# The copy ahead of the second slab's cast, other pairs in the first group, and sums called at the fetch, in a macaron encoder kernel

## The chip, the cores and the metric

The kernel runs on one core of a Trainium2 chip. The metric is device time in microseconds (us) of one execution. A core has TensorE (PE) for matmuls, VectorE (DVE), ScalarE (ACT), GpSimd (POOL) and SyncE (SP). Each engine works through its own list of instructions in order and waits for the others by semaphores. SP and POOL are used here to issue DMA transfers.

## What is computed

The reference is a two-layer encoder trunk. Each layer has a feed-forward block, a mixer and a second feed-forward block, so there are four feed-forward blocks, called (0,0), (0,1), (1,0) and (1,1) by layer and place. The change touches the feed-forward blocks alone:

```python
D_MODEL, SEQ, N_META, D_FF, DEPTH = 1024, 512, 16, 2816, 2

def swiglu(x, w_gate, w_up, w_down):
    return (jax.nn.silu(x @ w_gate) * (x @ w_up)) @ w_down

for l in range(DEPTH):
    h = h + 0.5 * swiglu(rmsnorm(h, norm_gains[l, 0]), ffn_w_gate[l, 0], ffn_w_up[l, 0], ffn_w_down[l, 0])
    h = h + mixer(...)
    h = h + 0.5 * swiglu(rmsnorm(h, norm_gains[l, 2]), ffn_w_gate[l, 1], ffn_w_up[l, 1], ffn_w_down[l, 1])
```

There are 528 tokens (16 of them learned), 512 behind the last mixer, so a half of the tokens is 264 or 256 columns.

## The kernel before

**Tiling.** The 2816 hidden channels are 22 chunks of 128, taken as 11 pairs. The pairs stand in groups of 4, 4 and 3 (`GROUPS`). Activations lie with channels on partitions and tokens along the row.

**Seven products instead of eight.** A pair's gate and up projections are written as a 2x2 block product and computed with seven products, named 1 to 7, in the order 1, 2, 6, 5, 7, 4, 3. Products 1, 2 and 4 use a weight block as it lies in memory, products 6, 5, 7 and 3 use sums of blocks. The down projections of the first two groups (`SEVENS = 2`) are done in the same way: `seven(g, what)` runs products 1, 6, 5, 7, 4, 2, 3 for two pairs of the group, the pairs whose hidden tensors were turned into the operand forms by `forms`. The group's other two pairs are multiplied plainly (`o22`, `o21`, `ea`, `eb`). The loads of such a group carry the numbers 11 and 12 (`NPAIR + g`). Each product is 24 matmuls.

**Weights.** A weight slab is a 128x1024 fp32 tile. SP fetches it into one of three `wraw` buffers. `make` turns it into two tiles: ACT casts it to `whi` (L305) and DVE subtracts to get the remainder `wlo` (L306), four buffers each. A matmul with full accuracy is three: hi by hi, hi by lo, lo by hi. Slabs that are sums are put together by `sums`: ACT writes a negative (`s`, L251), SP loads a plain block into a `wsb` buffer, and POOL issues DMAs that add onto a tile (L256). For the slab of product 6 there are two such additions, one behind the other: memory onto `s`, then `s` onto `w`.

**Partial sums.** A pair's quarters collect in the tile `c` (two buffers). After products 1, 6 and 7, `snapshot` copies the PSUM tile to `c` on ACT (L705), and the next product that adds onto that PSUM tile must wait for the copy. Products 2, 5 and 3 are added by DVE (L710). `hidden` then scales (L736, L739, DVE), applies silu (ACT L465), multiplies (L740), and either splits the result into hi and lo (`split`, L470 and L471) or, for the pairs in `SUMMED`, calls `forms` (ACT L755 and L764, DVE L756 to L765).

**The order at a group's end.** The last pair's product 7 is followed by the group's product 1, then by the pair's products 4 and 3, then by the group's products 6, 5, 7, `o22`, 4, `o21`, `ea`, 2, `eb` and 3. Product 4 adds onto the tile that the snapshot of product 7 reads. The additions to `h` (L803, DVE) take the group's results from PSUM.

The framework orders each engine's list by priority and readiness. `self.after(self.behind)` is a queueing rule alone: the cast is placed on ACT's list behind the instruction `behind`. Before the change it is used for one slab of block (0,0) and for the slabs in `RESERVED`.

In block (0,0) the first two pairs, 0 and 1, go through `first_pair` (eight plain products while the inputs arrive), and all their `hidden` steps run at once behind them.

Of the kernel before, what the change touches and what calls it, by code (L numbers as in the profile page):

```python
# [17 lines left out]
P = 128  # L18
# [15 lines left out]
SLAB = 1024  # L34
# [8 lines left out]
GROUPS = (4, 4, 3)  # L43
SEVENS = 2
# [19 lines left out]
RESERVED = [((l, f), 1, "5") for l, f in ((0, 1), (1, 0), (1, 1))]  # L64
SQUARES = {(0, "2"): (0, 1, 2, 3), (1, "1"): (4, 5, 6, 7)}
EARLIEST = ((0, 0), 2, "1")
SUMMED = [sum(GROUPS[:g]) + i for g in range(SEVENS) for i in range(2)]
LATE = KC - 3
PLACE = {p: i for i, p in enumerate("1256743")}
BLOCKS = ("11", "12", "21", "22")  # L70
# [3 lines left out]
NPAIR = FF // P // 2  # L74
# [143 lines left out]
class Weights:  # L218
# [58 lines left out]
    def fetch(self, upto):  # L277

        while self.fetched < min(upto, len(self.loads)):
            load = self.loads[self.fetched]  # L280
            if isinstance(load, int):
                w = self.raw.tile([P, SLAB], F32, tag="raw", name=f"raw{load}")
                self.nc.sync.dma_start(w, self.wts[load])
                self.raws[self.fetched] = w
            elif load[2] in DIRECT:
                w = self.raws[self.fetched] = self.block(*load[:2], DIRECT[load[2]])
                if load == EARLIEST:
                    self.sums(*load, w)
            self.fetched += 1

    def make(self, upto):
        nc = self.nc
        while self.made < min(upto, len(self.loads)):
            self.fetch(self.made + 1)
            s = self.made
            load = self.loads[s]
            w = self.raws.pop(s, None)
            if w is None:
                w = self.summed.pop(load)
            hi = self.hi_pool.tile([P, SLAB], F32R, tag="whi", name=f"whi{s}")  # L300
            lo = self.lo_pool.tile([P, SLAB], F32R, tag="wlo", name=f"wlo{s}")
            for a in np.split(np.arange(SLAB), 2 if s == 0 else 1):
                cs = slice(a[0], a[-1] + 1)
                with self.after(self.behind if load == ((0, 0), 2, "6") or load in RESERVED else None):
                    nc.scalar.copy(hi[:, cs], w[:, cs])  # L305
                nc.vector.tensor_tensor(lo[:, cs], w[:, cs], hi[:, cs].bitcast(F32), ALU.subtract)  # L306
            self.got[s] = (hi, lo)
            self.got.pop(s - 12, None)
            self.made += 1
            if not isinstance(load, int) and load[2] in ("1", "2") and load != EARLIEST:  # L310
                self.sums(*load, w)

    def use(self, j):
# [31 lines left out]
def build(tc, ctx, xt, wts, win, wdn, par, w2, const, umask, out):  # L345
# [118 lines left out]
    def act(*args, **kw):  # L464
        prev_act[0] = S.activation(*args, **kw).ins  # L465

    def split(src, tag_hi, tag_lo):
        n = src.shape[-1]
        hi, lo = slot(tag_hi, F32R, n), slot(tag_lo, F32R, n)
        S.copy(hi, src)  # L470
        V.tensor_tensor(lo, src, hi.bitcast(F32), ALU.subtract)  # L471
        return hi, lo
# [153 lines left out]
    def ffn(l, f, norm, done, following):  # L626

        x, rs, n = norm.x, None, live[0]
        w = n // 2
        pools = kept.pop() if kept else open_pools("left", psum=("s2",), c=2, gx=6, s2=2)  # L630
        made, hid, sums, formed, sevens = {}, {}, {}, {}, {}

        def second(p):
            return (p + f) % 2 == 0

        def quarters():
            return slots["c"].tile([P, 4 * T], F32, tag="c", name=nm("c"))[:, : 4 * n].rearrange("p (j q c) -> p j q c", j=2, q=4)
# [61 lines left out]
        def finished(p, product):  # L699
            st = made[p]  # L700
            acc = st[{"2": "Y", "5": "Z", "3": "Z"}.get(product, "X")][:, :, :w]

            def snapshot(q):
                with tc.high_priority():
                    snap = S.copy(st["c"][:, :, q], acc).ins  # L705
                if p == 0 and q == 3:
                    W.behind = snap

            def more(q, acc):
                V.tensor_tensor(st["c"][:, :, q], st["c"][:, :, q], acc, ALU.add)  # L710

            if product == "1":
                st["c"] = quarters()
                snapshot(0)
            elif product == "2":
                more(0, acc)
            elif product == "6":
                snapshot(1)
            elif product == "7":
                snapshot(3)  # L720
                more(3, st["Z"][:, :, :w])
            elif product == "4":
                hidden(st, p, 1)
            elif product == "3":
                more(1, acc)
                hidden(st, p, 0)

        def hidden(st, p, m):

            c = st["c"]  # L730
            t, u = [c[:, j, 2 * m : 2 * m + 2].rearrange("p q c -> p (q c)") for j in range(2)]
            x21 = st["X"][:, :, :w] if "X" in st else None
            cuts = [(t, u, t, u, slice(0, n))] if m == 0 or x21 is None else \
                [(t[:, :w], u[:, :w], x21[:, 0], x21[:, 1], slice(0, w)), (t[:, w:], u[:, w:], t[:, w:], u[:, w:], slice(w, n))]
            for td, _, ts, _, cs in cuts:
                V.scalar_tensor_tensor(td, ts, -0.5, rs[:, cs], ALU.mult, ALU.mult)  # L736
            act(t, t, AF.Silu)
            for _, ud, _, us, cs in cuts:
                V.scalar_tensor_tensor(ud, us, -0.25, rs[:, cs], ALU.mult, ALU.mult)  # L739
                V.tensor_tensor(ud, t[:, cs], ud, ALU.mult)  # L740
            if p in SUMMED:
                st["rows"] = st.get("rows", 0) + 1
                if st["rows"] == 2:
                    formed[p] = forms(c)
            else:
                hid[2 * p + m] = split(u, "g", "g")

        def forms(c):

            t, u = c[:, 0], c[:, 1]  # L750
            two = [[v2(slot(tag, F32R)) for _ in range(2)] for tag in ("g", "g", "gx")]
            last = v2(slot("gx", F32R))

            def parts(to, src):
                S.copy(to[0], src)  # L755
                V.tensor_tensor(to[1], src, to[0].bitcast(F32), ALU.subtract)  # L756

            parts(two[0], u[:, 0:4:2])
            V.tensor_tensor(t[:, 0:4:2], u[:, 1:2].broadcast_to([P, 2, w]), u[:, 0:4:3], ALU.subtract)
            V.tensor_tensor(t[:, 1], u[:, 3], t[:, 0], ALU.subtract)  # L760
            parts(two[1], t[:, 0:2])
            V.tensor_tensor(t[:, 3], u[:, 2], t[:, 1], ALU.subtract)
            parts(two[2], t[:, 2:4])
            S.activation(last[:, 0], u[:, 3], AF.Copy, scale=-1.0)  # L764
            V.scalar_tensor_tensor(last[:, 1], u[:, 3], -1.0, last[:, 0].bitcast(F32), ALU.mult, ALU.subtract)  # L765
            return [(hi[:, i], lo[:, i]) for hi, lo in two for i in range(2)] + [(last[:, 0], last[:, 1])]

        def seven(g, what):

            base, (left, right) = sum(GROUPS[:g]), (slice(0, w), slice(w, n))  # L770
            alone = second(base + GROUPS[g] - 1)
            st = sevens.setdefault(g, {})

            def weights(name):
# [6 lines left out]

            def times(to, half, name, wt, begin=False):
                hi, lo = wt
                for k in range(2):
                    xh, xl = formed[base + k][PLACE[name]]
                    for j in range(2):
                        for i, (a, b) in enumerate(((hi, xh), (hi, xl), (lo, xh))):
                            TE.matmul(to[:, j], a[:, 2 * half + j, k], b, start=begin and k == 0 and i == 0,  # L788
                                      stop=k == 1 and i == 2, skip_group_check=not begin)

            def plain(to, hs, wt, begin=False):
                hi, lo = wt
                for k in range(4):
                    xh, xl = hid[2 * base + 4 + k]
                    for j in range(2):
                        for i, (a, b) in enumerate(((hi, xh), (hi, xl), (lo, xh))):
                            TE.matmul(to[:, j], a[:, j, k], b[:, hs], start=begin and k == 0 and i == 0,  # L797
                                      stop=k == 3 and i == 2, skip_group_check=not begin)
# [14 lines left out]
            elif what == "5":  # L813
                wt = weights(what)
                for half in range(2):
                    z = acc("z", half, alone)
                    times(z, half, what, wt, True)
                    add(z, half, 0, right)
# [609 lines left out]
    first = Norm(G_NORM)  # L1428
# [16 lines left out]
    for l in range(DEPTH):  # L1445
        a, b, c = norms[3 * l : 3 * l + 3]
# [92 lines left out]
```

## Time and profile before

| | us |
|---|---|
| time, median of 3 runs | 2244.19 (2242.94 to 2246.18) |
| time of the profiled execution | 2241.11 |
| its span, first to last instruction | 2239.3 |
| PE busy / DVE busy / ACT busy | 2183.8 / 1611.1 / 1267.9 |
| PE idle behind ACT's copy at L705 | 37.1 in 9 waits |

The span is covered by the trace; 1.8 us of the profiled execution's time lie around it. Matmuls overlap in the pipe, so a matmul's own duration (287 ns) is longer than the distance from one to the next, and busy time of PE is not a measure of its speed. The granted clock of TensorE is given as a share: 1.00 is 2.4 GHz, 0.50 is 1.2 GHz.

### The profile page before, as it was taken

To read this page: it belongs to the slowest core of one execution; us is meant where nothing else is said; L and a number is where in the kernel's file an instruction comes from. 1 tells how busy PE (TensorE), PEld (TensorE's weight loads), DVE (VectorE), ACT (ScalarE), POOL (GpSimd) and SP (SyncE) were. 2 spreads that over 40 slices of the span, in tenths; PEclk is the share of its full clock that TensorE was granted. 3 is DMA by queue.
4 is the path that set the end of the run, shared out by engine and by line. 5 is a ranking of instruction groups with operands and counts; after the bars stand their busy time and mean duration, and the time that the engine had idled before them with its cause. 6 is when DMAs were issued, how large, how long until landed. Compare 5 with 4: busy or idle time off the path is not lost. (4 is left out here: it accounts for less than half of the span.)

```text
span 2239.3 us, 40811 instructions
## 1 busy us (share of the span) xinstructions
PE 2183.8 (98%) x16764; PEld 2104.0 (94%) x16764; DVE 1611.1 (72%) x2599; ACT 1267.9 (57%) x1892; POOL 175.6 (8%) x204
## 2 busy tenths in 40 slices
PE   9899999999999999999999999999999999899998
PEld 9899999999999999999998999999888889899997
DVE  7858567577876696685797586675889867768675
ACT  8546355354784574554585463554557937646454
POOL 1011110000000011111011111100000001111110
PEclk9999999999999999999999999999999999999999
DMA  8589673212114585878677796732221137878671
GB/s 247 144 214 220 156 180 114 83 60 63 42 38 128 137 225 155 223 170 209 175 187 193 192 223 160 189 117 82 75 67 48 66 113 179 217 187 229 165 193 66
DMA packets 93338, 332.05 MB, mean 148 GB/s; under 512 B 10336, under 2 KB 12640, under 8 KB 93152
## 3 DMA queue, kind: packets, MB, share of 16 engines
q1 hardware_dynamic: 62272, 221.35, 28.6%
q0 software_dynamic: 28800, 104.87, 26.3%
q10 hardware_dynamic: 2080, 3.23, 0.4%
q8 instruction: 131, 2.15, 0.4%
q14 instruction: 55, 0.45, 0.1%
HBM read 274.88 MB, written 2.10 MB: 124 GB/s over the span
## 5 line engine op out<-in xcount | busy, mean ns | idle before, releaser
L695 PE MATMUL ss<-xc,whi 128*128 128x264 f32 (+1 forms) x4608 | 853.1, 287 | 37.2 <-ACT c L705 37.1
L695 PEld LDWEIGHTS ss<-xc,whi 128*128 128x128 f32 x4608 | 725.1, 192 | 40.1 <-ACT c L705 39.6
L695 PE MATMUL ss<-xc,wlo 128*128 128x264 f32 (+1 forms) x2304 | 659.2, 286 | 0.0
L306 DVE TENSOR_TENSOR wlo<-w,whi 128x1024 fp32r<-128x1024 f32 (+1 forms) x259 | 315.2, 1217 | 207.8 <-ACT whi L305 207.3
L695 PEld LDWEIGHTS ss<-xc,wlo 128*128 128x128 f32 x2304 | 440.9, 191 | 0.0
L305 ACT CAST whi<-w 128x1024 fp32r<-128x1024 f32 (+1 forms) x259 | 269.9, 1045 | 229.5 <-PE ss L695 114.4
L482 PE MATMUL mm<-x,whi 128*128 128x264 f32 (+1 forms) x1712 | 383.3, 314 | 0.0
L482 PEld LDWEIGHTS mm<-x,whi 128*128 128x128 f32 x1712 | 278.2, 188 | 15.7 <-DVE x L471 0.2
L482 PE MATMUL mm<-x,wlo 128*128 128x264 f32 (+1 forms) x856 | 264.4, 313 | 0.0
L305 ACT CAST whi<-raw 128x1024 fp32r<-128x1024 f32 x126 | 132.0, 1048 | 152.6 <-PE mm L482 69.5
L306 DVE TENSOR_TENSOR wlo<-raw,whi 128x1024 fp32r<-128x1024 f32 x126 | 153.9, 1222 | 80.1 <-ACT whi L305 79.0
L797 PE MATMUL ss<-g,whi 128*128 128x264 f32 (+1 forms) x1024 | 186.6, 283 | 0.0
L251 ACT ACTIVATE s<-w 128x1024 f32<-128x1024 f32 x100 | 106.0, 1060 | 132.0 <-DMA w<-win 83.0
L306 DVE TENSOR_TENSOR wlo<-s,whi 128x1024 fp32r<-128x1024 f32 x100 | 122.2, 1222 | 71.9 <-ACT whi L305 70.7
L305 ACT CAST whi<-s 128x1024 fp32r<-128x1024 f32 x100 | 105.1, 1051 | 115.9 <-PE ss L695 75.6
L482 PEld LDWEIGHTS mm<-x,wlo 128*128 128x128 f32 x856 | 159.6, 188 | 7.4
L797 PEld LDWEIGHTS ss<-g,whi 128*128 128x128 f32 x1024 | 158.2, 188 | 0.0
L482 PE MATMUL ss<-g,whi 128*128 128x264 f32 (+1 forms) x828 | 153.1, 301 | 0.0
L797 PE MATMUL ss<-g,wlo 128*128 128x264 f32 (+1 forms) x512 | 145.0, 283 | 0.0
L482 PEld LDWEIGHTS ss<-g,whi 128*128 128x128 f32 x828 | 120.5, 188 | 5.2
L710 DVE TENSOR_TENSOR c<-c,ss 128x528 f32<-128x528 f32 (+1 forms) x126 | 87.8, 697 | 41.5 <-ACT c L705 33.2
L256 POOL DMA_DIRECT2D w<-win x42 | 37.0, 880 | 953.5 <-DVE g L1346 386.5
(314 smaller groups left out, 3900.4 us busy)
## 6 DMA issues: line engine op xcount, KB each, us to landing
w<-win SPq DMA_DIRECT2D x217, 512.0 KB, 5.5
raw<-wts SPq DMA_DIRECT2D x126, 512.0 KB, 3.5
w<-s POOLq DMA_DIRECT2D x50, 512.0 KB, 6.1
s<-w POOLq DMA_DIRECT2D x50, 512.0 KB, 7.1
w<-win POOLq DMA_DIRECT2D x42, 512.0 KB, 8.1
s<-win POOLq DMA_DIRECT2D x42, 512.0 KB, 6.2
w<-wdn SPq DMA_DIRECT2D x40, 512.0 KB, 4.4
woa<-wdn SPq DMA_DIRECT2D x8, 512.0 KB, 6.6
```

Source lines behind the costliest of these rows:

```text
L251: self.nc.scalar.activation(t, w, AF.Copy, scale=-1.0)
L256: self.nc.gpsimd.dma_start(t, src, accum_op=ALU.add)
L305: nc.scalar.copy(hi[:, cs], w[:, cs])
L306: nc.vector.tensor_tensor(lo[:, cs], w[:, cs], hi[:, cs].bitcast(F32), ALU.subtract)
L482: TE.matmul(acc.half[i][:width], lhs, rhs[:, acc.spans[i]], start=first, stop=last)
L695: TE.matmul(acc[:, j], a[:, j, k], b[:, at], start=bool(begin and k == 0 and i == 0), stop=k == len(x) - 1 and i == 2, skip_group_check=no ...
L710: V.tensor_tensor(st["c"][:, :, q], st["c"][:, :, q], acc, ALU.add)
L797: TE.matmul(to[:, j], a[:, j, k], b[:, hs], start=begin and k == 0 and i == 0, stop=k == 3 and i == 2, skip_group_check=not begin)
```

## The change

The diff has three edits. First, `fetch` calls `sums` for product 1 of the down projections' slabs, where `make` called it. Second, at the end of each of the first two groups of every block, `behind` is set to the copy of the last pair's product 7, and the cast of the slab of the group's product 6 is placed behind it on ACT. Third, in group 0 of block (0,0) the seven products take pairs 1 and 2 instead of 0 and 1, and pairs 0 and 3 are multiplied plainly; the weights in memory are laid out to match.

```diff
--- before.py
+++ after.py
@@ -64,7 +64,18 @@
 RESERVED = [((l, f), 1, "5") for l, f in ((0, 1), (1, 0), (1, 1))]
 SQUARES = {(0, "2"): (0, 1, 2, 3), (1, "1"): (4, 5, 6, 7)}
 EARLIEST = ((0, 0), 2, "1")
-SUMMED = [sum(GROUPS[:g]) + i for g in range(SEVENS) for i in range(2)]
+
+
+def summed_pairs(block, g):
+    first = sum(GROUPS[:g]) + (block == (0, 0) and g == 0)
+    return [first, first + 1]
+
+
+def plain_pairs(block, g):
+    base = sum(GROUPS[:g])
+    return [p for p in range(base, base + GROUPS[g]) if p not in summed_pairs(block, g)]
+
+
 LATE = KC - 3
 PLACE = {p: i for i, p in enumerate("1256743")}
 BLOCKS = ("11", "12", "21", "22")
@@ -284,7 +295,7 @@
                 self.raws[self.fetched] = w
             elif load[2] in DIRECT:
                 w = self.raws[self.fetched] = self.block(*load[:2], DIRECT[load[2]])
-                if load == EARLIEST:
+                if load == EARLIEST or load[1] >= NPAIR and load[2] == "1":
                     self.sums(*load, w)
             self.fetched += 1
 
@@ -294,6 +305,7 @@
             self.fetch(self.made + 1)
             s = self.made
             load = self.loads[s]
+            summed_first = not isinstance(load, int) and load[1] >= NPAIR and load[2] == "6"
             w = self.raws.pop(s, None)
             if w is None:
                 w = self.summed.pop(load)
@@ -301,13 +313,13 @@
             lo = self.lo_pool.tile([P, SLAB], F32R, tag="wlo", name=f"wlo{s}")
             for a in np.split(np.arange(SLAB), 2 if s == 0 else 1):
                 cs = slice(a[0], a[-1] + 1)
-                with self.after(self.behind if load == ((0, 0), 2, "6") or load in RESERVED else None):
+                with self.after(self.behind if load == ((0, 0), 2, "6") or load in RESERVED or summed_first else None):
                     nc.scalar.copy(hi[:, cs], w[:, cs])
                 nc.vector.tensor_tensor(lo[:, cs], w[:, cs], hi[:, cs].bitcast(F32), ALU.subtract)
             self.got[s] = (hi, lo)
             self.got.pop(s - 12, None)
             self.made += 1
-            if not isinstance(load, int) and load[2] in ("1", "2") and load != EARLIEST:
+            if not isinstance(load, int) and load[2] in ("1", "2") and load != EARLIEST and (load[1] < NPAIR or load[2] == "2"):
                 self.sums(*load, w)
 
     def use(self, j):
@@ -703,7 +715,7 @@
             def snapshot(q):
                 with tc.high_priority():
                     snap = S.copy(st["c"][:, :, q], acc).ins
-                if p == 0 and q == 3:
+                if q == 3 and (p == 0 or p + 1 in (sum(GROUPS[: g + 1]) for g in range(SEVENS))):
                     W.behind = snap
 
             def more(q, acc):
@@ -738,7 +750,7 @@
             for _, ud, _, us, cs in cuts:
                 V.scalar_tensor_tensor(ud, us, -0.25, rs[:, cs], ALU.mult, ALU.mult)
                 V.tensor_tensor(ud, t[:, cs], ud, ALU.mult)
-            if p in SUMMED:
+            if any(p in summed_pairs((l, f), g) for g in range(SEVENS)):
                 st["rows"] = st.get("rows", 0) + 1
                 if st["rows"] == 2:
                     formed[p] = forms(c)
@@ -767,8 +779,8 @@
 
         def seven(g, what):
 
-            base, (left, right) = sum(GROUPS[:g]), (slice(0, w), slice(w, n))
-            alone = second(base + GROUPS[g] - 1)
+            left, right = slice(0, w), slice(w, n)
+            alone = second(sum(GROUPS[: g + 1]) - 1)
             st = sevens.setdefault(g, {})
 
             def weights(name):
@@ -781,8 +793,8 @@
 
             def times(to, half, name, wt, begin=False):
                 hi, lo = wt
-                for k in range(2):
-                    xh, xl = formed[base + k][PLACE[name]]
+                for k, p in enumerate(summed_pairs((l, f), g)):
+                    xh, xl = formed[p][PLACE[name]]
                     for j in range(2):
                         for i, (a, b) in enumerate(((hi, xh), (hi, xl), (lo, xh))):
                             TE.matmul(to[:, j], a[:, 2 * half + j, k], b, start=begin and k == 0 and i == 0,
@@ -790,8 +802,8 @@
 
             def plain(to, hs, wt, begin=False):
                 hi, lo = wt
-                for k in range(4):
-                    xh, xl = hid[2 * base + 4 + k]
+                for k, c in enumerate(2 * p + i for p in plain_pairs((l, f), g) for i in range(2)):
+                    xh, xl = hid[c]
                     for j in range(2):
                         for i, (a, b) in enumerate(((hi, xh), (hi, xl), (lo, xh))):
                             TE.matmul(to[:, j], a[:, j, k], b[:, hs], start=begin and k == 0 and i == 0,
@@ -1499,14 +1511,14 @@
     for l in range(DEPTH):
         for f in range(2):
             for g in range(SEVENS):
-                p = sum(GROUPS[:g])
+                own, rest = summed_pairs((l, f), g), plain_pairs((l, f), g)
                 for row in range(2):
                     for c in range(2):
-                        parts.append(dn[l, f, p : p + 2, c, :, :, row].transpose(1, 2, 0, 3).reshape(P, SLAB))
+                        parts.append(dn[l, f, own][:, c, :, :, row].transpose(1, 2, 0, 3).reshape(P, SLAB))
                 for row in (1, 0):
                     for half in range(2):
                         js = slice(2 * half, 2 * half + 2)
-                        parts.append(dn[l, f, p + 2 : p + 4, :, :, js, row].transpose(2, 3, 0, 1, 4).reshape(P, SLAB))
+                        parts.append(dn[l, f, rest][:, :, :, js, row].transpose(2, 3, 0, 1, 4).reshape(P, SLAB))
     wdn = np.ascontiguousarray(np.stack(parts))
     par = np.zeros((P, NPAR), np.float32)
     par[:, G_NORM:G_GN] = a["norm_gains"].reshape(-1, P).T
```

**Where instructions stand.** All eight group ends change alike; this is ACT's list at the end of group 1 of block (0,0). `w_00_12_2569` is the slab of product 6 (`w_00_12_2499` in the changed kernel), `w_00_12_2572` that of product 5, `s_00_12_2566` that of product 7. Before:

```order
L470 CAST g_2604<-c_2175 128x528
L305 CAST whi_2667<-w_00_12_2569 128x1024
L705 COPY c_2428<-ss_2399 128x2x264
L305 CAST whi_2699<-w_00_12_2572 128x1024
L305 CAST whi_2740<-s_00_12_2566 128x1024
```

After:

```order
L482 CAST g_2604<-c_2175 128x528
L717 COPY c_2428<-ss_2399 128x2x264
L317 CAST whi_2667<-w_00_12_2499 128x1024
L317 CAST whi_2699<-w_00_12_2502 128x1024
L317 CAST whi_2740<-s_00_12_2496 128x1024
```

The copy of product 7 and the cast have changed places. DVE's list at the same place, before:

```order
L306 TENSOR_TENSOR wlo_2668<-w_00_12_2569,whi_2667 128x1024
L803 TENSOR_TENSOR h<-h,ss_2671 128x2x264
L710 TENSOR_TENSOR c_2428<-c_2428,ss_2608 128x2x264
L803 TENSOR_TENSOR h<-h,ss_2685 128x2x264
L306 TENSOR_TENSOR wlo_2700<-w_00_12_2572,whi_2699 128x1024
L736 SCALAR_TENSOR_TENSOR c_2428<-c_2428,rs_711 128x264
L739 SCALAR_TENSOR_TENSOR c_2428<-c_2428,rs_711 128x264
```

After:

```order
L722 TENSOR_TENSOR c_2428<-c_2428,ss_2608 128x2x264
L748 SCALAR_TENSOR_TENSOR c_2428<-c_2428,rs_711 128x264
L815 TENSOR_TENSOR h<-h,ss_2671 128x2x264
L318 TENSOR_TENSOR wlo_2668<-w_00_12_2499,whi_2667 128x1024
L815 TENSOR_TENSOR h<-h,ss_2685 128x2x264
L318 TENSOR_TENSOR wlo_2700<-w_00_12_2502,whi_2699 128x1024
L751 SCALAR_TENSOR_TENSOR c_2428<-c_2428,rs_711 128x264
```

Three small instructions now stand ahead of the subtraction for slab 6: the addition to `c`, one scaling and one addition to `h`.

In block (0,0), behind the first two pairs, ACT's list before reads as follows (`c_310` is pair 0, `c_566` pair 1, `c_847` pair 2; `g_774` to `gx_780` are the forms of pair 0):

```order
L305 CAST whi_819<-w_00_2_639 128x1024
L755 CAST g_774<-c_310 128x528
L305 CAST whi_850<-w_00_3_649 128x1024
L305 CAST whi_887<-s_00_2_338 128x1024
L755 CAST g_776<-c_310 128x528
L755 CAST gx_778<-c_310 128x528
L465 ACTIVATE c_566<-c_566 128x528
L764 ACTIVATE gx_780<-c_310 128x264
L705 COPY c_847<-ss_818 128x2x264
```

After (`c_837` is pair 2):

```order
L482 CAST g_770<-c_310 128x528
L317 CAST whi_809<-w_00_2_639 128x1024
L482 CAST g_778<-c_310 128x528
L317 CAST whi_840<-w_00_3_649 128x1024
L477 ACTIVATE c_566<-c_566 128x528
L717 COPY c_837<-ss_808 128x2x264
```

Two instructions for pair 0 are gone, and one cast of a slab has moved behind the copy. At the end of that group the forms of pair 2 appear around the cast of slab 6 (`whi_1221`); after:

```order
L767 CAST g_1144<-c_837 128x528
L717 COPY c_972<-ss_943 128x2x264
L317 CAST whi_1221<-w_00_11_1043 128x1024
L767 CAST g_1146<-c_837 128x528
L767 CAST gx_1148<-c_837 128x528
L317 CAST whi_1253<-w_00_11_1046 128x1024
L776 ACTIVATE gx_1150<-c_837 128x264
```

Where before ACT had the cast, the copy and the next cast there, three of the four instructions of the forms on ACT now stand behind the cast of slab 6. On SP and POOL every row keeps its place, and so do all ACT rows at L251, which the first edit is about; the lists of the changed kernel are the same on all five engines with the first edit and without it.

## Rows read from the trace of the kernel before

**Rows 1.** The page's head: span, busy time, share of the span and instructions by engine.

```profile
span 2239.3 us, 40811 instructions
PE 2183.8 (98%) x16764; PEld 2104.0 (94%) x16764; DVE 1611.1 (72%) x2599; ACT 1267.9 (57%) x1892; POOL 175.6 (8%) x204
```

**Rows 2.** Waits of PE: engine, line, releaser; us in total, times, longest.

```profile
PE ss L695 <- ACT c L705: 37.1, 9, 6.0
PE ss L1057 <- DVE t L1066: 2.0, 2, 1.0
```

**Rows 3.** Timeline of PE: start, us, instruction, [idle before <- releaser]; five of nine waits.

```profile
64.58 0.51 PE L695 MATMUL ss<-xc,whi 128*128 128x264 f32 x2 [3.86 <-ACT c L705]
...
101.35 0.51 PE L695 MATMUL ss<-xc,whi 128*128 128x264 f32 x2 [3.08 <-ACT c L705]
...
230.50 0.81 PE L695 MATMUL ss<-xc,whi 128*128 128x264 f32 x2 [3.24 <-ACT c L705]
...
1957.82 0.58 PE L695 MATMUL ss<-xc,whi 128*128 128x256 f32 x1 [5.98 <-ACT c L705]
...
2085.99 0.39 PE L695 MATMUL ss<-xc,whi 128*128 128x256 f32 x1 [3.26 <-ACT c L705]
```

**Rows 4.** Windows of 9 us behind the nine waits: us, engines busy, PEclk, DMA.

```profile
64.58:73.58 9.00, 9.00 (x61) 9.00 (x62) 8.61 (x12) 5.55 (x8) 0.88 (x1) 0.81 0.42 125
101.35:110.35 9.00, 9.00 (x73) 9.00 (x74) 8.97 (x16) 4.84 (x6) 0.88 (x1) 1.00 0.20 61
230.50:239.50 9.00, 9.00 (x52) 9.00 (x53) 7.33 (x13) 2.85 (x4) 0.88 (x1) 0.68 0.18 60
862.11:871.11 9.00, 9.00 (x53) 9.00 (x54) 7.44 (x13) 2.96 (x4) 0.86 (x1) 0.69 0.17 60
993.96:1002.96 9.00, 9.00 (x61) 9.00 (x62) 8.34 (x14) 3.90 (x5) 0.44 (x1) 0.81 0.19 60
1224.03:1233.03 9.00, 9.00 (x53) 9.00 (x54) 7.45 (x13) 2.97 (x4) 0.86 (x1) 0.70 0.18 58
1356.23:1365.23 9.00, 9.00 (x63) 9.00 (x64) 8.55 (x15) 4.10 (x6) 0.88 (x1) 0.84 0.17 58
1957.82:1966.82 9.00, 9.00 (x55) 9.00 (x56) 7.52 (x13) 3.10 (x4) 0.86 (x1) 0.69 0.17 59
2085.99:2094.99 9.00, 9.00 (x63) 9.00 (x64) 8.37 (x15) 4.07 (x6) 0.86 (x1) 0.81 0.18 58
```

**Rows 5.** Waits of ACT for a DMA, then ACT's timeline at 228 us.

```profile
ACT whi L305 <- DMA w<-s: 54.2, 8, 8.5
...
228.90 1.04 ACT L305 CAST whi<-w 128x1024 fp32r<-128x1024 f32 x1 [5.91 <-DMA w<-s]
229.85 0.59 ACT L705 COPY c<-ss 128x528 f32<-128x528 f32 x1
```

**Rows 6.** Windows behind the copy at 230 us: the third busy time is DVE's.

```profile
229.98:234.84 4.86, 4.34 (x19) 4.34 (x20) 4.86 (x7) 1.41 (x2) 0.00 (x0) 0.50 0.02 3
236.19:236.99 0.80, 0.80 (x8) 0.80 (x8) 0.77 (x2) 0.80 (x2) 0.00 (x0) 0.99 0.81 328
237.09:245.43 8.34, 8.34 (x71) 8.34 (x70) 8.09 (x13) 4.83 (x7) 0.88 (x1) 1.00 0.39 64
```

**Rows 7.** Block (0,0) behind pairs 0 and 1: timeline of DVE and ACT.

```profile
57.83 1.32 DVE L740 TENSOR_TENSOR c<-c 128x528 f32<-128x528 f32 x2
...
63.47 0.42 DVE L765 SCALAR_TENSOR_TENSOR gx<-c,gx 128x264 fp32r<-128x264 f32 x1
...
63.92 0.60 ACT L705 COPY c<-ss 128x528 f32<-128x528 f32 x1 [0.66 <-DVE gx L765]
```

**Rows 8.** Block (0,0), end of group 0: the cast of slab 6, and POOL's additions.

```profile
99.76 1.04 ACT L305 CAST whi<-w 128x1024 fp32r<-128x1024 f32 x1 [5.72 <-DMA w<-s]
...
84.14 1.23 POOL L256 DMA_DIRECT2D s<-wdn  x1
95.11 0.87 POOL L256 DMA_DIRECT2D w<-s  x1 [9.74 <-DMA s<-wdn]
```

## Prediction

> **What bounds the kernel now.** Read the head of the page first [rows 1]: PE is busy for 2183.8 of 2239.3 us, and no other engine comes near. So time is won only where PE stands still or runs slowly. The waits of PE say where it stands still [rows 2]: 37.1 us in nine waits, all at product 4 or a like product for ACT's copy at L705; the next entry is 2.0 us. The timeline places them [rows 3]: one at 64.58 us, behind the first two pairs of block (0,0), and eight at the ends of the groups with seven products, two in each block, of 3.08 to 5.98 us. Then read the granted clock behind each wait [rows 4]. In eight of the nine windows of 9 us it is 0.68 to 0.84 instead of 1.00: for 2.9 to 5.8 us TensorE runs at its lower level, 1.2 GHz, although it is busy throughout. A wait here costs its idle time and, behind it, 9 x (1 - clock) us of work not done. Only the wait of 3.08 us, at 101.35, has 1.00 behind it.
>
> Why does the copy come late? ACT's own waits show it [rows 5]: eight casts wait 54.2 us together for the DMA that adds `s` onto `w`, which is slab 6. At 228 us the cast stands ahead of the copy, waits 5.91 us for the landing, and the copy runs 0.95 us behind the cast's start. Its source, product 7, had long been done. PE needs the copy at once, and slab 6 two products later.
>
> **The first edit** (sums called at the fetch) moves nothing: no row of ACT, POOL or SP changes place through it. I cost it at 0, and no cover is needed.
>
> **The second edit, at seven group ends** (all but the first of block (0,0)). Three terms.
>
> *Waits that go.* Behind the swap the copy needs product 7 alone, which ends while PE still works through the group's product 1. So 37.1 - 3.86 - 3.08 = 30.2 us of idle time go [rows 2, 3].
>
> *Clock that stays up.* The seven windows from 230.50 on give 9 x (0.32 + 0.31 + 0.19 + 0.30 + 0.16 + 0.31 + 0.19) = 16.0 us [rows 4].
>
> *What is late next.* The landing of slab 6 does not move. At 230.50 it lay 1.70 us ahead of PE's restart (228.80, 0.10 ahead of the cast), that is, a wait of i us has the landing i - 1.7 us behind the moment at which product 4 could have begun; call this T. DVE begins slab 6's subtraction 1.18 us behind the landing (229.98, where the first window begins) [rows 6]. From there to the end of the subtraction for `o22` it had 4.86 + 0.77 + 8.09 = 13.7 us of work in the three windows [rows 6]. Three of these instructions now stand ahead of it (an addition to `c`, one to `h`, a scaling), about 0.62 + 0.62 + 0.35 us by their spacing, which leaves 12.1. So that tile is ready at T + i - 1.7 + 1.2 + 12.1 = T + i + 11.6. PE comes there behind five products (4, 3, 6, 5, 7) of 24 matmuls at 0.12 us (8.34 us for 71, a row at full clock [rows 6]), 14.4 us, and needs the remainder at its third matmul, T + 14.6. What remains of each wait is therefore i - 3.0 us: from 0.2 us (i = 3.24) to 3.0 us (i = 5.98). Over the seven this is 30.2 - 7 x 3.0 = 9.2 us, a queue on DVE where it had been a wait for ACT. It should come in pieces: product 5 needs PSUM that DVE's additions to `c` give back, `o22` the subtraction. Slab 6 itself is subtracted at T + i + 0.7 and wanted at T + 6.0, so it is late only by 0.7 us in the worst place, and this is within the 3.0.
>
> Queued behind the copy on ACT are the casts of slabs 6, 5 and 7. None could start before the landing or before PE gives buffers back, so the copy costs them nothing; its cover is the wait for the landing itself. Should the landing come before product 7 ends, the cast would be late by the 0.59 us of the copy.
>
> Sum: 30.2 + 16.0 - 9.2 = 37.0 us.
>
> **The third edit, in block (0,0).** *Behind the first pairs.* The wait of 3.86 us ends with a copy at 63.92 that waits for the last reader of pair 0's tile, DVE's instruction at 63.47, the last of the forms [rows 7]. With pair 0 split plainly, DVE's list from 57.83 has five instructions of that size up to the last reader, at their spacing of 0.62 us: 60.9. One silu stands between on ACT, then the copy of 0.60: done at 61.9 instead of 64.5. So 2.6 us of the 3.86 go, and 1.3 remain. The lower clock behind it cost 9 x 0.19 = 1.7 us [rows 4], and I take it as gone. Together 4.3 us. Bounds: 0 if another reader holds the tile, 3.86 + 1.7 = 5.6 if the copy is early enough.
>
> *At the end of group 0.* The 3.08 us go, with no clock to win. But the forms of pair 2 now lie there: behind the cast of slab 6 ACT has two casts of forms, the cast of slab 5 and one more form, and DVE's subtraction for slab 6 stands behind the last of them. That puts 1.04 + 2 x 0.6 + 1.0 + 0.4 + 0.35 = 4.0 us between the landing and the subtraction, where elsewhere there are 1.2. The landing was at 99.66 [rows 8]. It can move by 0 to 4.3 us with PE; I take 3.4, near the upper end, since its chain starts at casts and subtractions that run earlier too. T then is 101.35 - 3.08 - 4.3 = 94.0, and the landing 2.3 us behind it. Here both additions to `h` stand ahead, so DVE's work is 12.1 - 0.6 = 11.5, and the tile for `o22` is ready at T + 2.3 + 4.0 + 11.5 = T + 17.8 against T + 14.6: 3.2 us late. The last split of pair 3 lies four small instructions and a subtraction further down DVE's list, about 4.2 us, where PE has 2.8 us of matmuls to do: 1.4 us more. So 4.6 us of new waits stand against 3.1: a loss of 1.5 us. If the landing does not move, the loss is 4.9; if nothing is late, a gain of 3.1.
>
> **The sum.** 37.0 + 4.3 - 1.5 = 39.8 us. The profiled execution took 2241.1 us, 1.8 around its span; the change makes it 2201.3. The median of the runs lies 3.1 us above the profiled execution, so I predict 2204 us. With no new wait anywhere, the gain is 30.2 + 16.0 + 4.3 + 3.1 = 53.6 us: 2191.
>
> **The rivals.**
>
> *The clock falls again.* If the remaining waits at seven group ends draw the lower clock as the old ones did, the 16.0 us are not won, and the time is 2220. For it: eight of nine waits here had it behind them. Against: the one of 3.08 us did not [rows 3, 4], and what remains is at most 3.0 us, cut into pieces. Chance 0.13, with cases where only the longest places are hit.
>
> The Trainium skill ("TensorE: Matmul & The Clock Gate", section on HAM oscillation) tells of a kernel whose matmul bursts, parted by waits, start again at the lower clock each time. Taken for every wait that is left, it would give this rival's 24 us of gain; the row at 101.35 shows a wait that did not do it, and gives the 40. The trace agrees with the page for the eight others.
>
> *DVE keeps up.* The remaining waits came from one place's DVE windows, in which DVE itself had small gaps. If its queue drains faster, up to 9.2 + 4.6 us more are won: 2191 to 2197. Against: its list is fixed, and its instructions' times too. Chance 0.10.
>
> *The landings come later: slower.* The old waits gave the DMAs rest: their share behind a wait is 0.17 to 0.20 [rows 4]. A PE that runs on asks for slabs sooner, and the additions are sensitive to company: the one issued at 84.14 let the next go at 95.11 only, 11 us, while that next one took 4.6 us (landed 99.66) [rows 8]. Each us by which all eight landings come later costs 8 us. Slower by over 0.2% needs 39.8 + 4.5 = 44.3 us; with the 16.0 us of clock lost again, 28.3 us are left, 3.5 us at each landing. That is the point from which it decides; at 5 us each the time is 2220 + 40 = 2260. Chance 0.04.
>
> *The change does too little.* If slab 6's landing drifts so far that the wait only goes from product 4 to product 6, 5.8 us further on, less than 4.5 us is won. The landings at i - 1.7 = 1.5 to 4.3 us behind T speak against it. Chance 0.03.
>
> **The numbers.** 0.2%, about 4.5 us, is what a measurement of this kernel can tell from no change. The forecast's own range is 2197 to 2212, with chance 0.70. With the bounds of full gain and of the lost clock the range is 2191 to 2220. Faster 0.93, same 0.03, slower 0.04.
>
> **What the profile after would show.** PE's waits for the copy are down to one, of about 1.3 us near 60 us. Windows behind the seven places show a clock of 1.00. New small waits of PE stand at the groups' products 5 and 6 and `o22`, with DVE named, longest in the first groups of blocks (0,1), (1,0) and (1,1). ACT's casts still wait for the DMA onto `w`, with about the same sum. The prediction is wrong if PE waits over 3 us at product 6, if the low clock is still there, or if POOL's additions land later against PE than before.

## The result, and the profile after

The changed kernel takes 2205.11 us (median of 4 runs, 2201.77 to 2209.43) against 2243.57 us before (4 runs): a ratio of 0.9832, 95% interval 0.9808 to 0.9855. The forecast was 2204 us. The execution that was profiled is the longest of the four, 2209.43 us with a span of 2207.6.

The head of the page, against [rows 1]: PE's busy time fell by 8 us, and the span by 32.

```profile
span 2207.6 us, 40817 instructions
PE 2175.4 (99%) x16764; PEld 2092.4 (95%) x16764; DVE 1607.7 (73%) x2599; ACT 1266.6 (57%) x1892; POOL 175.2 (8%) x204
```

PE's waits, against [rows 2] (us in total, times, longest). The 37.1 us for ACT's copy are gone from the head of the list; small entries with DVE named and one for the cast `whi` stand there:

```profile
PE ss L800 <- ACT whi L317: 3.1, 2, 2.3
PE ss L809 <- DVE h L815: 2.9, 4, 1.2
PE ss L800 <- DVE wlo L318: 2.1, 3, 0.8
...
PE ss L800 <- DVE c L722: 1.9, 4, 0.7
```

PE's timeline at three places, against [rows 3]: behind the first pairs; at the end of group 0 of block (0,1); and of block (1,1), where before there was one wait of 5.98 us.

```profile
60.48 0.51 PE L707 MATMUL ss<-xc,whi 128*128 128x264 f32 x2 [0.59 <-ACT whi L317]
61.54 0.52 PE L707 MATMUL ss<-xc,whi 128*128 128x264 f32 x2 [0.55 <-ACT c L717]
...
880.07 0.40 PE L809 MATMUL ss<-g,whi 128*128 128x264 f32 x2
880.31 0.28 PE L809 MATMUL ss<-g,wlo 128*128 128x264 f32 x1
881.61 0.49 PE L809 MATMUL ss<-g,whi 128*128 128x264 f32 x2 [1.01 <-DVE h L815]
...
1930.64 0.51 PE L800 MATMUL ss<-g,whi 128*128 128x256 f32 x2 [2.34 <-ACT whi L317]
1931.90 0.39 PE L800 MATMUL ss<-g,wlo 128*128 128x256 f32 x1 [0.75 <-DVE wlo L318]
```

Windows of 9 us at six of the nine places of [rows 4] (PEclk stands third from the end): the first pairs, the ends of both groups of (0,0), of group 0 of (0,1), and of both groups of (1,1). The lower level is left at one place. A last window shows a stretch of it in the first mixer, where before there was none.

```profile
60.48:69.48 9.00, 8.45 (x66) 8.24 (x67) 9.00 (x13) 6.52 (x10) 0.27 (x1) 1.00 0.63 164
100.44:109.44 9.00, 8.36 (x66) 8.15 (x67) 8.97 (x16) 4.57 (x6) 0.88 (x1) 1.00 0.43 93
228.73:237.73 9.00, 9.00 (x76) 8.97 (x75) 8.96 (x16) 5.39 (x7) 0.88 (x1) 1.00 0.52 117
855.35:864.35 9.00, 8.26 (x66) 7.87 (x65) 8.97 (x16) 4.37 (x7) 0.86 (x1) 1.00 0.37 86
...
1928.30:1937.30 9.00, 5.90 (x35) 5.70 (x35) 6.64 (x11) 5.13 (x6) 0.00 (x0) 0.81 0.26 74
2056.81:2065.81 9.00, 6.66 (x49) 5.92 (x48) 8.20 (x14) 5.94 (x8) 0.86 (x1) 1.00 0.18 60
...
560.00:564.00 4.00, 4.00 (x22) 3.85 (x22) 1.77 (x4) 1.92 (x5) 0.00 (x0) 0.57 0.00 0
```

ACT at the end of group 0 of (1,1), against [rows 5], and POOL's additions there. The copy now runs at once, and the cast behind it still waits for the DMA onto `w`. On POOL the first row is slab 5's addition: it waits 11.18 us for its own block, and the two additions of slab 6 stand behind it.

```profile
1919.82 0.59 ACT L717 COPY c<-ss 128x512 f32<-128x512 f32 x1 [1.26 <-PE ss L707]
1929.55 1.99 ACT L317 CAST whi<-w 128x1024 fp32r<-128x1024 f32 x2 [9.14 <-DMA w<-s]
...
1913.28 0.87 POOL L267 DMA_DIRECT2D w<-wdn  x1 [11.18 <-DMA w<-wdn]
1913.83 1.23 POOL L267 DMA_DIRECT2D s<-wdn  x1
1924.97 0.87 POOL L267 DMA_DIRECT2D w<-s  x1 [9.90 <-DMA s<-wdn]
```

POOL works through its list in order, so the first wait holds up the additions of slab 6: the next issue comes 0.55 us behind its end. The Trainium skill ("DMA: Bandwidth & Descriptors", section "Anatomy of one DMA — SWDGE (gpsimd) path") states that a DMA's semaphore wait happens on the sequencer that issues it, before dispatch. These rows agree with it.

### The profile page after: what moved, and what is told of

It is laid out like the page before. It is cut to its first block, busy times and chain, and to the rows that moved or that the text cites. A ratio compares the mean times of both kernels' runs of the same rounds, so it can differ in the third digit from the quotient of the medians.

```text
span 2207.6 us, 40817 instructions
## 1 busy us (share of the span) xinstructions
PE 2175.4 (99%) x16764; PEld 2092.4 (95%) x16764; DVE 1607.7 (73%) x2599; ACT 1266.6 (57%) x1892; POOL 175.2 (8%) x204
## 4 chain that ended last, share of the span: by engine, by line
PE 79%; DVE 9%; DMA 5%; ACT 4%; issue 3%; POOL 0%; DVEq 0%; ACTq 0%; POOLq 0%; SPq 0%
PE ss L707 32%; PE mm L494 12%; PE ss L494 11%; PE ss L809 7%; PE ss L800 4%; PE sm L494 3%; DMA s<-wdn 2%; PE ss L662 2%; DVE wlo L318 2%; DMA w<-s 1%; ACT t L477 1%; PE sm L1226 1%; DVE h L815 1%; ACT whi L317 1%; PE ss L689 1%
## 5 line engine op out<-in xcount | busy, mean ns | idle before, releaser
L707 PE MATMUL ss<-xc,whi 128*128 128x264 f32 (+1 forms) x4608 | 837.2, 283 | 1.1 <-ACT whi L317 0.6
L707 PEld LDWEIGHTS ss<-xc,whi 128*128 128x128 f32 x4608 | 712.4, 188 | 2.4 <-ACT c L717 1.3
L707 PE MATMUL ss<-xc,wlo 128*128 128x264 f32 (+1 forms) x2304 | 652.3, 283 | 0.0
L707 PEld LDWEIGHTS ss<-xc,wlo 128*128 128x128 f32 x2304 | 433.4, 188 | 0.0
```

The source lines that it names most:

```text
L707: TE.matmul(acc[:, j], a[:, j, k], b[:, at], start=bool(begin and k == 0 and i == 0), stop=k == len(x) - 1 and i == 2, skip_group_check=no ...
```

## The experiments

The theory at this point: slab 6's late landing is the cause of the waits, ACT's list only handed them to the copy, and the lower clock follows a PE that stands still. The first four kernels shared one chip, with before at 2245.33 us (13 runs). The last two shared another, with before at 2243.74 us (12 runs).

**The second edit alone.** Before, with these lines (and the two functions of the third edit, which here return the old pairs):

```diff
+            summed_first = not isinstance(load, int) and load[1] >= NPAIR and load[2] == "6"
-                with self.after(self.behind if load == ((0, 0), 2, "6") or load in RESERVED else None):
+                with self.after(self.behind if load == ((0, 0), 2, "6") or load in RESERVED or summed_first else None):
-                if p == 0 and q == 3:
+                if q == 3 and (p == 0 or p + 1 in (sum(GROUPS[: g + 1]) for g in range(SEVENS))):
```

> The kernel before with the second edit alone: the cast of slab 6 behind the copy of product 7 at all eight group ends. Theory (waits for a copy that stands behind a late cast, and the lower clock behind them): 37.0 us at the seven group ends and 3.0 us at the end of group 0 of block (0,0), where the forms of pair 2 do not lie; the wait of 3.86 us at 64.6 us with its low clock stays. Ratio to the kernel before near 0.982, that is within 0.2% of the whole change. Rival (the first group's pairs carry a good part of the gain): a ratio of 0.987 or more.

Measured: 2211.91 us, ratio 0.9846 (0.983 to 0.9863), 33.4 us less than before. PE's waits:

```profile
PE ss L809 <- DVE h L815: 4.3, 6, 1.8
PE ss L707 <- ACT c L717: 3.9, 1, 3.9
PE ss L800 <- ACT whi L317: 3.6, 2, 3.1
```

The one wait for the copy left is that behind the first pairs. The interval lies between the theory's 0.982 and the rival's 0.987. This edit carries most of the change, and the long remainder is again in group 0 of (1,1): 3.13 us for the cast at product 6, at 1936.47.

**The third edit alone.** Before, with `summed_pairs` and `plain_pairs` as in the change:

```diff
+    first = sum(GROUPS[:g]) + (block == (0, 0) and g == 0)
```

> The kernel before with the third edit alone: pairs 1 and 2 in the first group's products. Theory: the wait at 64.6 us shrinks from 3.86 to about 1.2 us and the low clock behind it goes, 4.3 us won; at the end of group 0 the wait for the copy stays or grows by about 1 us, since product 4 comes earlier than the landing of slab 6 does, and the forms of pair 2 behind the cast cost 1 to 4 us more; a low clock there would cost 1.7 us. So 0 to 4 us in all, a ratio of 0.998 to 1.001; the seven other ends keep waits of 3.2 to 6.0 us. Rival (the third edit matters by itself): 0.995 or less.

Measured: 2240.36 us (10 runs), ratio 0.9975 (0.9961 to 0.9989), 5.0 us less, a little more than the theory's 0 to 4 and less than the rival's. The seven other ends keep waits of 2.51 to 6.91 us. The wait behind the first pairs is 0.59 + 0.55 us as in the changed kernel, with clock 1.00 behind it; but the wait at the end of group 0 of (0,0), 3.19 us, now has the lower level behind it. Windows behind both:

```profile
60.48:69.48 9.00, 8.41 (x66) 8.20 (x67) 9.00 (x13) 6.52 (x10) 0.24 (x1) 1.00 0.66 170
96.96:105.96 9.00, 9.00 (x61) 9.00 (x62) 8.97 (x16) 5.14 (x8) 0.00 (x0) 0.81 0.19 60
```

**The order of the additions, on before.** POOL's addition for slab 5 is queued behind both additions of slab 6. The lists of ACT, DVE and SP keep every row, so the copy still stands behind the cast:

```diff
-        self.nc.gpsimd.dma_start(t, src, accum_op=ALU.add)
+        return self.nc.gpsimd.dma_start(t, src, accum_op=ALU.add).ins
-            self.add(s2, s3)
+            second = self.add(s2, s3)
-            self.add(s1, self.dram(f, i, "22"))
+            with self.after(second if i >= NPAIR else None):
+                self.add(s1, self.dram(f, i, "22"))
```

> The kernel before, with one thing moved on POOL: at the two groups of each block the addition for slab 5 is queued behind the second addition for slab 6, so that memory onto s, and s onto w, come first. ACT's cast of slab 6 stays ahead of the copy. Theory (the wait is the landing of slab 6, and the place of the cast on ACT only hands it on to PE): slab 6 lands 5 to 8 us earlier, ahead of the end of product 7, so all eight waits for the copy go, 33.3 us, with 16.0 us of low clock: ratio about 0.978, better than the whole change, and no wait moves to product 6 or to the plain products. Slab 5 then lands about 3 us later than slab 6, before product 5 wants it. Rival (the DMA engines are the limit, not the order of the additions): the landing moves by under 2 us, waits of 2 to 4 us stay, ratio 0.985 or more.

Measured: 2201.62 us, ratio 0.9801 (0.9786 to 0.9816). The copy's waits fall from 37.1 us in nine to 8.4 us in four, the longest that behind the first pairs:

```profile
PE ss L696 <- ACT c L706: 8.4, 4, 3.9
```

Not all eight waits at the group ends go: 2.99 and 1.31 us are left in the two groups of (1,1), and 0.24 in (0,1). Counted against product 4, slab 6 lands 2 to 5.3 us earlier than before, where 5 to 8 were expected, and the ratio is a little above the theory's 0.978. The rival's 0.985 lies outside the interval. So the landing is the cause, and ACT's order only says who pays for it. An early landing alone wins at least as much as the whole change.

**The same order, on the change.**

> The changed kernel with the same move on POOL. Theory: what is left at the group ends is set by the landing of slab 6 (its subtraction opens DVE's queue), so PE's waits at products 6 and 5 and at the plain products, 12.3 us in all in the profile of the changed kernel, go with it, and the one low stretch of clock behind them (1.7 us): about 14 us won, ratio to the kernel before 0.976 to 0.978. Rival (DVE's queue is the limit by its own length): the waits stay, ratio 0.982 to 0.984.

Measured: 2191.61 us (2189.00 to 2195.35), ratio to before 0.9758 (0.9741 to 0.9775): 53.7 us less than before on the same chip, and the fastest version here. POOL and ACT at the end of group 0 of (1,1):

```profile
1898.38 0.87 POOL L267 DMA_DIRECT2D s<-wdn  x1 [6.54 <-ACT s L262]
1906.29 0.89 POOL L267 DMA_DIRECT2D w<-s  x1 [7.03 <-DMA w<-wdn]
1906.90 1.17 POOL L267 DMA_DIRECT2D w<-wdn  x1
...
1911.88 1.05 ACT L318 CAST whi<-w 128x1024 fp32r<-128x1024 f32 x1 [1.03 <-DMA w<-s]
```

The cast waits 1.03 us instead of 9.14, and no wait of PE longer than 0.3 us is left at any group end. Only the program's end still has the lower level.

**PE kept busy in the wait.** Before, with the second half of each group's product 1 computed three times over, 24 more matmuls ahead of product 4 (the result is the same). ACT, POOL and SP keep every row; on DVE, unlike what was expected, four rows at each group end change places (an addition to `h`, two scalings and slab 6's subtraction):

```diff
-                    times(x, half, what, wt, what == "1")
+                    for _ in range(3 if what == "1" and half else 1):
+                        times(x, half, what, wt, what == "1")
```

> The kernel before, with the second half of each group's product 1 computed three times over (the accumulation starts anew each time, so the result is the same): 24 more matmuls of about 0.12 us, 2.9 us, that PE does at each of the eight group ends just ahead of product 4. No other engine's list changes. There they lie inside the wait for ACT's copy, which is 3.1 to 6.0 us long. Theory (a PE that stands still for some 3 us and more draws the lower clock, and this is a term of its own, 16.0 us in the sum): the copy's waits fall from 37.1 to about 14 us in all, none but the two long ones of the first groups and the first one near 64 us above 2 us, the end of product 4 is where it was, the windows behind have clock 1.00, and 12 to 16 us are won although PE has 23 us more work: 2229 to 2233. Rival (the lower clock comes with the place, not with the standing still, or costs nothing that isn't waited for later): within 3 us of before, 2242 to 2248. Second rival (the 24 matmuls delay the copy or DVE's addition and so add to the path): slower, up to 2268.

Measured: 2234.22 us, ratio 0.9956 (0.9943 to 0.9969): 9.5 us less, with 192 more matmuls, where 12 to 16 were expected. The copy's waits are 15.1 us in eight, so 22.0 us of idle time gave way to about 23 us of work. What was won is the clock. Windows behind five of the nine places, whose waits were 3.86, 0.55, 2.53, 2.31 and 3.66 us:

```profile
64.70:73.70 9.00, 9.00 (x54) 9.00 (x55) 8.34 (x11) 4.77 (x7) 0.08 (x1) 0.70 0.38 118
...
232.03:241.03 9.00, 8.99 (x73) 9.00 (x74) 8.93 (x16) 4.78 (x6) 0.44 (x1) 1.00 0.18 58
862.48:871.48 9.00, 9.00 (x63) 9.00 (x64) 8.66 (x15) 4.12 (x6) 0.44 (x1) 0.84 0.17 58
...
1221.14:1230.14 9.00, 9.00 (x74) 9.00 (x75) 8.93 (x16) 4.80 (x7) 0.36 (x1) 1.00 0.18 58
...
1951.66:1960.66 9.00, 9.00 (x53) 9.00 (x54) 7.41 (x13) 2.90 (x4) 0.46 (x1) 0.67 0.19 61
```

The rival that the clock costs nothing falls, and so does the one that the matmuls add to the path. By the windows behind the nine places, 9 x (1 - clock) falls from 17.7 us in [rows 4] to 2.7 + 1.4 + 3.0 = 7.1 us. A new stretch at 1.2 GHz in the first mixer, 3.4 us at 568 us, takes 1.7 us of this back: 8.9 us, against 9.5 measured. Two of the eight group ends kept the lower level, group 0 of (0,1) and group 0 of (1,1), the first with a wait of only 2.53 us; the window behind the first pairs, which got no matmuls, lost 1.0 us more than in [rows 4].

**The order of the additions and the second edit, without the third.**

> The whole change with POOL's addition for slab 5 queued behind slab 6's two, but without the third edit (pairs 0 and 1 are again the ones turned into forms in the first group). Theory (the third edit acts behind the first pairs alone, by 3.86 - 1.14 us of wait and 1.7 to 3.4 us of low clock; at the end of group 0 it costs nothing once the landing is early): the wait of 3.9 us near 64 us comes back with low clock around it, nothing else, and the time is 4 to 6 us above that of the version with all edits and this order, 2196 to 2198. Rival (the third edit is worth only what it gave when made alone at those waits' expense elsewhere, or PE catches up at a later wait): less than 2 us above, 2192 to 2193.6.

Measured: 2197.82 us, ratio 0.9796 (0.9778 to 0.9814), 6 to 8.5 us above the version with all edits (by the medians, or by the ratios, as the chips differ). The wait of 3.86 us is back (at 64.32, with a clock of 0.75 behind it). But against the theory there is more: 3.2 us in four waits for DVE's `h` at L810, where the version with all edits had 0.6 in two, and a stretch at 1.2 GHz at 560 us, 1.7 us, that the other does not have. Why these come back is open.

## Why the prediction came out

**The copy's waits and the second edit.** The mechanism was right: 30.2 us of waits went, and a queue on DVE came in their place. It was forecast at 9.2 us over seven places, from 0.2 us to 3.0 each. The timeline shows 9.8 us, but otherwise shared out: 1.2 at 253 us, in group 1 of (0,0), 1.8 in group 0 of (0,1), nothing in its group 1, 0.5 in (1,0), then 3.5 and 2.7 in the two groups of (1,1). The total is right by luck, because two errors cancel: (1,1) has 6.3 us where 3.3 were forecast, the five other places 3.5 where 5.9 were.

**The step that failed: "The landing of slab 6 does not move."** Counted from the moment at which product 4 can begin (its start less its wait), the trace's DMA records give for the landing, in us:

| end of group | before | after | POOL's order, all edits |
|---|---|---|---|
| (0,0) 0 / 1 | 1.4 / 1.6 | 1.7 / 1.6 | -2.3 / -2.3 |
| (0,1) 0 / 1 | 3.3 / 1.8 | 3.2 / 1.2 | 1.8 / -2.3 |
| (1,0) 0 / 1 | 3.7 / 2.2 | 3.0 / 1.8 | -1.8 / -2.7 |
| (1,1) 0 / 1 | 4.3 / 1.6 | 7.0 / 5.4 | -1.1 / 1.0 |

In six places it holds within 0.8 us. In (1,1) it slips by 2.7 and 3.9 us, which is the rival "The landings come later" in two places of eight. A landing at 7.0 and a cast that is done 1.1 us later come to 8.1, and product 6 wants the slab at 5.8: the 2.34 us at 1930.64. In group 0 the same slip stands in the second edit's own run (7.8 us, wait 3.13) and not in the third edit's (4.3), so there it goes with the second edit. In group 1 it does not: the second edit's run has 5.1, but the third edit's run, whose lists are as before in that block, has 5.2 as well, with a copy's wait of 6.91 us. With one trace of each kernel, what moved that landing stays open. The slip has two parts in group 0: the addition onto `s` is issued 1.8 us later against PE (8.6 us ahead of product 4, where it was 10.4), and it takes longer: from its issue to the next one's are 11.1 us, before 10.2. The point at which this rival decides, 3.5 us at all eight, was far off; the landings of all eight moved by 0.6 us on average. The rival's ground, that an addition of 11 us had suffered from its company, is not borne out: ahead of slab 5's addition, with POOL's order, the one onto `s` still took up to 10.9 us to the next issue.

Of the three signs that the prediction named for being wrong, the first did not come (PE's longest wait at product 6 is 2.34 us), the second came at one place of seven, and the third in (1,1). ACT's casts wait 43.5 us for the DMA onto `w`, less than the 54.2 that were to stay.

**The clock.** Forecast: 16.0 us at seven places, and 1.7 behind the first pairs. Six of the seven and the first pairs have 1.00. The seventh, at 1928.30, loses 1.7 us, just where the landing slipped, and the stretch at 560 us costs 4 x 0.43 = 1.7 us that no step foresaw. So 14.3 of the 17.7 us were won. That this is a term of its own was shown by the run with PE kept busy.

**The third edit.** Behind the first pairs 1.14 us of wait were left where 1.3 were forecast. At the end of group 0 of (0,0) PE waits 0.62, 0.64 and 1.04 us, 2.3 in all, where 4.6 were forecast: a gain of 0.8 instead of a loss of 1.5. The landing there, 1.7 us behind the moment at which product 4 can begin (2.3 forecast), and the subtraction 3.9 us behind it (4.0 forecast) were near; what stands in DVE's queue behind them cost PE less than was worked out. The edit gave 5.0 us alone and 6 to 8.5 with POOL's order; 2.8 were forecast, so this term was too small: by the rows it is 2.7 + 1.7 + 0.8 = 5.2 us.

**The first edit** was costed at nothing, since no row changes place through it; no run has it alone.

**The sum.** 39.8 us were forecast and 38.5 measured between the medians. The two profiled executions are 31.7 us apart. Their rows give: waits of PE above 0.15 us, 45.5 to 21.6, 23.9 us; clock 14.3; together 38.2. Term by term this is the forecast's 39.8, less 3.4 of clock and 0.6 of waits behind the second edit, plus 2.4 of waits that the third edit saved beyond its forecast. That it comes so near is in part luck, as these errors offset each other. Against the 38.2 stands that a wait cut into pieces costs more than its idle time. At 880.31 one matmul starts, and the next at 881.61: 1.30 us later instead of 0.12, so 1.18 are lost where the row says 1.01, and the start behind it comes 0.08 us late as well. At 0.25 us each, an estimate from this one wait, ten more waits than before cost 2.5 us. The other 4 us between rows and spans can't be placed; the profiled execution lies 4.3 us above its median.

## What to carry to other kernels

When an engine waits for a copy whose source has long been done, read what stands ahead of the copy and what that waits for: moving the copy wins the wait, but the late transfer is still late, and the next reader pays a part of it. Then look at the queue of that transfer: here an addition that waited for its own block stood ahead of two that were wanted sooner, and changing their order won as much as the whole change, and 13 to 17 us on top of it. Count the lower clock behind PE's waits as a term of its own, and don't take the place of a landing over from a trace in which the waits that go had given the transfers their time.

## What was not expected of the hardware

- Between 1.8 and 3.1 us, the length of a single wait does not tell whether the lower clock follows. Waits of 2.51 and 2.80 us had it behind them in the run of the third edit (0.81 in both windows), one of 2.53 us in the run with PE kept busy, and one of 1.77 us at 255.53 in the run of the second edit (0.85 from 250 to 259 us). Waits of 2.31 us with PE kept busy, 2.99 us with POOL's order on before, and 3.08 us in [rows 4] did not. The 20 waits of 3.09 us and more in the eight profiles here all had it behind them.
- The lower level also came at 560 us in the first mixer, among instructions that the change does not touch; PE waits 1.1 us in all in the 60 us around it, as it did before. Just ahead of it PE ran sixteen matmuls of 2 columns (1.00 us from 557.35, 0.95 from 559.25). Four of the six experiments have the same stretch behind the same matmuls, at 560 to 568 us; before, the third edit alone and POOL's order on the change do not. What decides is open.
- Issued 0.55 us behind slab 5's, the addition onto `s` took 8.1 to 11.1 us to the next issue at the eight group ends of the changed kernel. Issued ahead of it, it still took 6.9 to 10.9. What POOL's order gains is thus mostly the start: 14.5 to 16.6 us ahead of product 4 everywhere, against 8.6 to 13.4.
